# A hybrid decoder block on one core: the layout of the index phase and of the first attention's output changed, and all probability scaling of the second attention put on VectorE

## The chip, the cores and the metric

The kernel runs on one core of one Trainium2 chip. The core has five engines with a queue of their own each: TensorE (PE; its weight loads are listed as PEld), VectorE (DVE), ScalarE (ACT), GpSimd (POOL) and SyncE (SP), which here issues most DMAs. The metric is the device time of one execution in microseconds (us). Three runs of the kernel before took 1447.71 to 1451.23 us, with a median of 1449.72 us.

## The reference

One layer with 512 tokens of width 1024 in float32. The normalized input `h` goes through one wide projection, whose columns feed three token mixers and three gates. Each mixer's output is projected, gated and added to the input; then a two-layer network follows.

```python
h = rms_norm(x, norm1_g[l])
u = h @ w_in[l]
(dq, dk, dv, iq, ik, iw, nq, nkv, ng, sz, sxbc, sdt, mg) = jnp.split(u, offsets, axis=-1)
y_a = dsa_mixer(...)      # 16 heads of 64, one key/value head; an index score keeps 128 of the keys
y_b = nsa_mixer(...)      # 16 heads in 2 groups: compressed, selected and window attention, gated
y_c = ssd_mixer(...)      # 32 heads of a Mamba-2 recurrence in chunks of 128
mix = sig(g_A) * (y_a @ w_br_dsa) + sig(g_B) * (y_b @ w_br_nsa) + sig(g_C) * (y_c @ w_br_ssd)
x = x + mix @ w_out[l]
x = x + jnp.square(jax.nn.relu(rms_norm(x, norm2_g[l]) @ w_ff1[l])) @ w_ff2[l]
```

In the first attention each row's softmax `p = exp(s - max) / sum` multiplies `v`. In the second the same is done for the window and the selected blocks, and each is multiplied by a gate besides.

## The kernel before

All large products are made of three TensorE products of a high and a low half: `w = whi + wlo`, `h = hTh + hTl`, and the small product of the two low halves is dropped (L316 to L318). A weight tile of 128 rows by up to 1024 columns is loaded (`wraw`), ACT makes `whi` (L150), and DVE subtracts to give `wlo` (L151). There are 212 of these; three `wraw` and six `whi`/`wlo` are in flight, and tiles are prepared three ahead.

Two streams of work are interleaved. The main stream is: the index phase (which keys each token keeps), the first attention (DSA, 16 units of four heads by 128 queries), the recurrence (SSD), and the second attention (NSA, 32 units: 16 pairs of a window unit and a selection unit). Next to it a filler of projections supplies TensorE: `nkv`, `dq` (first-attention queries), `z`, `x`, `nq` (second-attention queries), 24 gate projections `mg`, and then the branches `a0, a1` (of y_a), `c0, c1` (of y_c), `b0, b1` (of y_b), each of four or eight `y` tiles times one weight half. After that `w_out` and the two layers of the network follow alone. The main stream books time for what it issues, and the filler is advanced until the debt is paid (`main`, `step`); a scheduler with a simulated time line then sets the order on each engine. Each engine runs its instructions in that order, and an instruction that waits holds up all behind it.

An attention unit takes these steps. Scores `sc` (L752, L753) are masked and their row maxima taken on DVE (L754); ACT makes `p = exp(...)` with the row sums (L761); DVE takes the reciprocal `rc` (L767), in NSA times the gate (L769); then `p` is scaled by `rc`, heads 0 to 2 on DVE (L774) and head 3 on POOL (L772). TensorE transposes `p` (L788), ACT and DVE make halves of it (L792, L793), and `pv` collects p times v (L800, L801). The values are laid out so that rows 0 to 63 of `pv` hold one half product and rows 64 to 127 the other; they are added as ACT copies the upper rows (L807) and DVE adds the lower ones (L808), and `yt` is stored (L809) into `ya_d` or `yb_d` in DRAM.

The branches read it back with `load_y`: SP loads `yr` (L663), ACT makes `yh` (L664), and POOL makes `yl` (L665; for `b1` DVE). `yr` comes from the tag `gt` with TG = 2 buffers, which rotate in program order and also hold `gth`, the gates' tanh (L632), stored by L633. The query blocks are transposed into `pF`; ACT and DVE make halves of 64 by 256 (L472, L473), and two DMAs of 256 KB store them in `q_d`, from which a POOL-issued DMA loads `qu` (L833).

## Time and profile before

| | before |
|---|---|
| median of three runs | 1449.72 us |
| profiled execution | 1447.78 us |
| its span, first to last instruction | 1446.1 us |
| PE busy | 1392.2 us (96%) |
| DVE busy | 973.5 us (67%) |
| ACT busy | 707.0 us (49%) |
| POOL busy | 300.1 us (21%) |
| mean granted TensorE clock | 0.982 of full speed |

The durations below are from the profiled execution, whose time is 1.7 us over its span. PE's matmuls are pipelined and their ends modelled, so that a PE shown as busy is not always at its peak: 1440 matmuls of the last 330 us take 0.229 us each, while a stretch with busy PE and slower matmuls is still listed as busy. So the number of matmuls in a stretch is read beside its busy time. The share of DVE differs greatly from stage to stage.

### The profile page before, as it was taken

Reading aid. Unit: us, or ns where it says so; the run is one execution under the profiler, and the core shown is the slowest. Engines: PE = TensorE matmul, PEld = TensorE weight load, DVE = VectorE, ACT = ScalarE, POOL = GpSimd, SP = SyncE. Lnnn points to the kernel's source line nnn. Section 1 sums busy time; section 2 is a strip of 40 time slices with the busy share of each in tenths; the row PEclk is TensorE's granted clock in tenths of the full one; section 3 lists DMA queues with packets and bytes.
Section 4 is the critical chain, followed back from the end, with each engine's and each line's share of the span. In section 5 each row is a group of like instructions: output and inputs, shape, how many; then the busy total and the mean of one; then the engine's idle time right before and its main releaser. Section 6 shows DMA issues by size and latency. Waiting matters only on the chain.

```text
span 1446.1 us, 19744 instructions
## 1 busy us (share of the span) xinstructions
PE 1392.2 (96%) x6832; PEld 1150.7 (80%) x6832; DVE 973.5 (67%) x1944; ACT 707.0 (49%) x1468; POOL 300.1 (21%) x270
## 2 busy tenths in 40 slices
PE   6999999999999989999999989998899999999998
PEld 5887778878878778788888777886679888888887
DVE  5699986888867776457578899787646443434331
ACT  4555335757756676546456446556424432413220
POOL 1021100111016767321035334252000000000000
PEclk9999999999999999999999999997899999999999
DMA  6334465454366778662277434242544323333231
GB/s 200 87 103 117 152 191 163 127 136 121 99 186 204 220 232 247 196 191 80 74 219 206 137 106 117 70 121 70 188 140 110 95 88 92 113 87 106 70 109 51
DMA packets 218273, 195.92 MB, mean 135 GB/s; under 512 B 15664, under 2 KB 165564, under 8 KB 218172
## 3 DMA queue, kind: packets, MB, share of 16 engines
q1 hardware_dynamic: 212700, 183.12, 42.8%
q0 software_dynamic: 4608, 8.39, 2.1%
q10 hardware_dynamic: 864, 3.15, 0.6%
q8 instruction: 54, 0.88, 0.3%
q14 instruction: 47, 0.39, 0.1%
HBM read 157.85 MB, written 36.77 MB: 135 GB/s over the span
## 4 chain that ended last, share of the span: by engine, by line
PE 67%; DVE 13%; DMA 9%; issue 4%; ACT 3%; POOL 3%; SPq 1%; DVEq 0%; POOLq 0%; ACTq 0%
PE pj L316 18%; PE pj L317 18%; PE pj L318 18%; DMA gld<-g_d 3%; DVE wlo L151 2%; PE pT L788 2%; PE sc L753 2%; PE sc L752 1%; DVE p L774 1%; PE pv L801 1%; PE pv L800 1%; DVE p L754 1%; DMA wraw<-in_w_in_dram 1%; DMA E<-ac_d 1%; ACT p L761 1%
## 5 line engine op out<-in xcount | busy, mean ns | idle before, releaser
L151 DVE TENSOR_TENSOR wlo<-wraw,whi 128x1024 fp32r<-128x1024 f32 (+3 forms) x212 | 257.1, 1216 | 133.3 <-ACT whi L150 124.1
L150 ACT ACTIVATE whi<-wraw 128x1024 fp32r<-128x1024 f32 (+3 forms) x212 | 207.8, 985 | 273.4 <-PE pj L317 118.5
L316 PE MATMUL pj<-hTh,whi 128*128 128x512 f32 x384 | 156.2, 407 | 0.9 <-DVE cacc L681 0.7
L318 PE MATMUL pj<-hTh,wlo 128*128 128x512 f32 x384 | 155.5, 405 | 0.0
L317 PE MATMUL pj<-hTl,whi 128*128 128x512 f32 x384 | 153.8, 401 | 0.0
L761 ACT ACTIVATE p<-p,nb,rs 128x256 f32<-128x256 f32 (+3 forms) x192 | 123.2, 644 | 58.8 <-DVE nb L759 58.8
L316 PE MATMUL pj<-whi,hTh 128*128 128x512 f32 (+2 forms) x352 | 139.5, 397 | 5.1 <-ACT qraw L458 1.7
L318 PE MATMUL pj<-whi,hTl 128*128 128x512 f32 (+2 forms) x352 | 137.9, 392 | 0.0
L317 PE MATMUL pj<-wlo,hTh 128*128 128x512 f32 (+2 forms) x352 | 137.5, 391 | 0.0
L316 PE MATMUL pj<-yh,whi 128*128 128x512 f32 x256 | 102.8, 405 | 5.0 <-ACT yh L664 3.0
L317 PE MATMUL pj<-yl,whi 128*128 128x512 f32 x256 | 102.7, 401 | 0.3 <-POOL yl L665 0.2
L318 PE MATMUL pj<-yh,wlo 128*128 128x512 f32 x256 | 101.7, 398 | 0.0
L316 PE MATMUL pj<-whi,fh 128*128 128x512 f32 x256 | 99.6, 389 | 0.0
L317 PE MATMUL pj<-wlo,fh 128*128 128x512 f32 x256 | 99.6, 389 | 0.0
L318 PE MATMUL pj<-whi,fo 128*128 128x512 f32 x256 | 99.6, 389 | 0.0
L317 PE MATMUL pj<-h2l,whi 128*128 128x512 f32 (+1 forms) x256 | 96.3, 376 | 0.0
L318 PE MATMUL pj<-h2h,wlo 128*128 128x512 f32 (+1 forms) x256 | 96.2, 376 | 0.0
L316 PE MATMUL pj<-h2h,whi 128*128 128x512 f32 (+1 forms) x256 | 96.1, 376 | 0.0
L772 POOL TENSOR_TENSOR p<-p,rc 128x256 f32<-128x256 f32 (+3 forms) x48 | 40.1, 835 | 230.3 <-DVE rc L767 88.3
L316 PEld LDWEIGHTS pj<-hTh,whi 128*128 128x128 f32 x384 | 73.0, 190 | 17.7 <-issue 2.4
L318 PEld LDWEIGHTS pj<-hTh,wlo 128*128 128x128 f32 x384 | 72.7, 189 | 16.5 <-issue 2.2
L1369 DVE TENSOR_TENSOR x<-x,pj 128x512 f32<-128x512 f32 x32 | 22.0, 686 | 93.5 <-PE pj L318 93.5
(332 smaller groups left out, 3153.0 us busy)
## 6 DMA issues: line engine op xcount, KB each, us to landing
wraw<-in_w_in_dram SPq DMA_DIRECT2D x84, 512.0 KB, 4.6
wraw<-in_w_ff_dram SPq DMA_DIRECT2D x64, 512.0 KB, 4.1
gld<-g_d SPq DMA_DIRECT2D x48, 256.0 KB, 3.5
q_d<-qev SPq DMA_DIRECT2D x32, 256.0 KB, 3.2
qu<-q_d POOLq DMA_DIRECT2D x32, 256.0 KB, 4.2
E<-ac_d SPq DMA_DIRECT2D x16, 512.0 KB, 4.9
wraw<-in_w_br_ssd_dram SPq DMA_DIRECT2D x16, 512.0 KB, 4.3
g_d<-gth SPq DMA_DIRECT2D x24, 256.0 KB, 2.4
```

The costliest lines, as they stand in the source:

```text
L150: act.activation(hi[:, :m], r[:, :m], AF.Copy)
L151: dve.tensor_tensor(lo[:, :m], r[:, :m], f(hi[:, :m]), op=ALU.subtract)
L316: pe.matmul(o, lh, rh, start=first, stop=False)
L317: pe.matmul(o, lh, rl, start=False, stop=False)
L318: pe.matmul(o, ll, rh, start=False, stop=last)
L752: pe.matmul(s_[:, h % w, :n], u.q[:, h], kh[:, :n], start=True, stop=False)
L753: pe.matmul(s_[:, h % w, :n], u.q[:, h], kl[:, :n], start=False, stop=True)
L754: dve.tensor_tensor_reduce(p_[:, h % w, :n], s_[:, h % w, :n], u.mask, 1.0, -3.4e38, ALU.add, ALU.max, accum_out=u.mx[:, h:h + 1])
L761: act.activation(u.p[h][:, :n], u.p[h][:, :n], AF.Exp, bias=u.nb[:, h:h + 1], scale=rs8[:, u.b, u.h0 + h:u.h0 + h + 1], accum_out=u.sm[:, ...
L772: pool.tensor_tensor(u.p[h][:, :n], u.p[h][:, :n], bc(rc[:, h:h + 1], [128, n]), op=ALU.mult)
L788: pe.transpose(pt[:, h], u.p[h][:, kb * 128:kb * 128 + 128], ident)
L1369: dve.tensor_tensor(x2s, x2s, p, op=ALU.add)
```

## The change

What it does, part by part:

1. The low halves `wlo` of the first 24 weight tiles (the first projection, `nkv`, `dq` and `z0`) are made on POOL instead of DVE.
2. A query block is evicted by one ACT copy and one DVE subtraction of 128 by 512 per (o, t), instead of four and four of 64 by 256. Eight DMAs of 64 rows and 512-byte pieces write it instead of two of 128 rows (16 blocks).
3. The output of the first attention is stored unscaled and unadded: ACT copies all of `pv` (128 by 512), and two DMAs write the two halves to `ya_d` and `ya2_d`. The same holds for group 0 of the second attention (`yb_d`, `yb2_d`). The DVE addition is gone there.
4. The first attention's `p` is not scaled. The reciprocals are gathered in `RC`, transposed at its end and stored in `rc_d` (`rc_out`).
5. `load_y` pays for this: for `a0`, `a1` and `b0` a POOL-issued accumulating DMA adds the second half into `yr`; for `a0` and `a1` a tile `yR` of the same tag `gt` is loaded with the reciprocals (two DMAs of 64 rows), and DVE multiplies. `yl` is made on DVE for every branch.
6. The second attention scales all four heads on DVE.
7. `ssd_prelude` is called after `nkv` instead of inside the index phase.

```diff
--- before.py
+++ after.py
@@ -24,8 +24,8 @@
 NS = 6
 RAWB = 3
 LEAD = 3
+NP = 24
 WE = 2
-SPL = {"a0": 1, "a1": 1, "c0": 1, "c1": 1, "b0": 1, "b1": 0}
 NH = 4
 BH = 2
 PTB, YTB, PGB = 3, 1, 1
@@ -78,6 +78,8 @@
     ac_d = scratch("ac_d", [128, 128])
     yc_d = scratch("yc_d", [2048, S])
     rs_d = scratch("rs_d", [4, 128])
+    rc_d = scratch("rc_d", [64, 128])
+    y2_d = {"a": scratch("ya2_d", [D, S]), "b": scratch("yb2_d", [D // 2, S])}
 
 
     cp = popen("const")
@@ -148,7 +150,7 @@
             hi = wp.tile([128, 1024], F32R, name="whi", tag="whi", bufs=NS)
             lo = wp.tile([128, 1024], F32R, name="wlo", tag="wlo", bufs=NS)
             act.activation(hi[:, :m], r[:, :m], AF.Copy)
-            dve.tensor_tensor(lo[:, :m], r[:, :m], f(hi[:, :m]), op=ALU.subtract)
+            (pool if i < NP else dve).tensor_tensor(lo[:, :m], r[:, :m], f(hi[:, :m]), op=ALU.subtract)
             s.hl[i] = (hi[:, :m].rearrange("p (a b) -> p a b", b=w), lo[:, :m].rearrange("p (a b) -> p a b", b=w))
             s.nsplit += 1
 
@@ -464,14 +466,16 @@
                 pt = ps("pF", [128, 4, 128])
                 for k in range(4):
                     pe.transpose(pt[:, k], raw[:, 128 * k:128 * k + 128], ident)
-                for j in range(2):
-                    ev = stg.tile([128, 2, 2, 128], F32R, name="qev", tag="ev", bufs=EB)
-                    pj = pt[:, 2 * j:2 * j + 2]
-                    for i in range(2):
-                        own, other = slice(64 * i, 64 * i + 64), slice(64 - 64 * i, 128 - 64 * i)
-                        act.activation(ev[own, :, i], pj[own], AF.Copy)
-                        dve.tensor_tensor(ev[other, :, i], pj[own], f(ev[own, :, i]), op=ALU.subtract)
-                    nc.sync.dma_start(q_d[2 * o + j][t], f(ev).rearrange("p a b c -> p (a b c)"))
+                qh = stg.tile([128, 4, 128], F32R, name="qev", tag="ev", bufs=EB)
+                ql = stg.tile([128, 4, 128], F32R, name="qev", tag="ev", bufs=EB)
+                act.activation(qh, pt, AF.Copy)
+                dve.tensor_tensor(ql, pt, f(qh), op=ALU.subtract)
+                for i in range(2):
+                    own, other = slice(64 * i, 64 * i + 64), slice(64 - 64 * i, 128 - 64 * i)
+                    for j in range(2):
+                        dst = q_d[2 * o + j][t].rearrange("r (a i c) -> r a i c", a=2, i=2)
+                        for e, rows in ((qh, own), (ql, other)):
+                            nc.sync.dma_start(dst[rows, :, i], f(e[own, 2 * j:2 * j + 2]))
                 if t == NB - 1:
                     done.add(f"q{o}")
             defer(0, tr)
@@ -661,8 +665,16 @@
         l_ = yp.tile([128, S], F32R, name="yl", bufs=4)
         src = yc_d if br[0] == "c" else y_d[br[0]]
         nc.sync.dma_start(yr, src[kk * 128:kk * 128 + 128])
+        if br[0] == "a" or br == "b0":
+            pool.dma_start(yr, y2_d[br[0]][kk * 128:kk * 128 + 128], accum_op=ALU.add)
+        if br[0] == "a":
+            R = gp.tile([128, S], F32, name="yR", tag="gt", bufs=TG)
+            for i in range(2):
+                a = rc_d[8 * kk + 4 * i:8 * kk + 4 * i + 4]
+                nc.sync.dma_start(R[64 * i:64 * i + 64], bass.AP(tensor=a.tensor, offset=a.offset, ap=[[0, 64], [1, S]]))
+            dve.tensor_tensor(yr, yr, R, op=ALU.mult)
         act.activation(h_, yr, AF.Copy)
-        (pool if SPL[br] else dve).tensor_tensor(l_, yr, f(h_), op=ALU.subtract)
+        dve.tensor_tensor(l_, yr, f(h_), op=ALU.subtract)
         return h_, l_
 
     def first_ya():
@@ -709,7 +721,6 @@
         for t in range(1, NB):
             IQ[t] = ix.tile([128, 8, 128], F32R, name=f"iqT{t}")
         yield "ik"
-        sv = yield from ssd_prelude()
         for b in range(1, NB):
             yield f"iq{b}"
             n = 128 * (b + 1)
@@ -731,7 +742,6 @@
             MASK[b] = wk
         MASK[0] = caus[:, 384:]
         pclose("idx")
-        return sv
 
 
     class U:
@@ -761,17 +771,26 @@
             act.activation(u.p[h][:, :n], u.p[h][:, :n], AF.Exp, bias=u.nb[:, h:h + 1],
                            scale=rs8[:, u.b, u.h0 + h:u.h0 + h + 1], accum_out=u.sm[:, h:h + 1])
 
+    RC = {}
+
+    def rc_out():
+        p = ps("pT", [128, 4, 128])
+        pe.transpose(p[:64, 0], RC["t"].rearrange("p a b -> p (a b)"), ident)
+        rt = gp.tile([128, S], F32, name="rct", tag="gt", bufs=TG)[0:64, 0:128]
+        act.activation(rt, p[:64, 0], AF.Copy)
+        nc.sync.dma_start(rc_d, rt)
+
     def a2(u):
         n = 128 * (u.b + 1)
+        if u.gate is None:
+            dve.reciprocal(RC["t"][:, u.h0:u.h0 + 4, u.b], u.sm)
+            return
         rc = at.tile([128, 4], F32, name="rc", bufs=3)
         dve.reciprocal(rc, u.sm)
         if u.gate is not None:
             dve.tensor_tensor(rc, rc, u.gate, op=ALU.mult)
         for h in range(4):
-            if h == 3:
-                pool.tensor_tensor(u.p[h][:, :n], u.p[h][:, :n], bc(rc[:, h:h + 1], [128, n]), op=ALU.mult)
-            else:
-                dve.tensor_scalar(u.p[h][:, :n], u.p[h][:, :n], rc[:, h:h + 1], None, op0=ALU.mult)
+            dve.tensor_scalar(u.p[h][:, :n], u.p[h][:, :n], rc[:, h:h + 1], None, op0=ALU.mult)
 
     def b1(u, ratio):
         nb = u.b + 1
@@ -801,7 +820,12 @@
                 pe.matmul(o, vk, pl0, start=False, stop=en)
                 yield ratio * 432
             prev = (kb, ph, pl)
-        if u.last:
+        if u.last and u.ydst2 is not None:
+            yt = at.tile([128, 4, 128], F32, name="yt", bufs=YTB)
+            act.activation(yt.rearrange("p a b -> p (a b)"), o, AF.Copy)
+            nc.sync.dma_start(u.ydst, yt[0:64])
+            nc.sync.dma_start(u.ydst2, yt[64:128])
+        elif u.last:
             yt = at.tile([64, 4, 128], F32, name="yt", bufs=YTB)
             ytf = yt.rearrange("p a b -> p (a b)")
             act.activation(ytf, o[64:128], AF.Copy)
@@ -833,8 +857,8 @@
         pool.dma_start(q.rearrange("p a b -> p (a b)"), q_d[hb][b])
         return q
 
-    def y_dst(which, h0, b):
-        t = y_d[which]
+    def y_dst(which, h0, b, ys=y_d):
+        t = ys[which]
         a = t[h0 * 64:(h0 + 4) * 64, b * 128:(b + 1) * 128]
         return a.rearrange("(h d) q -> d h q", d=64)
 
@@ -846,6 +870,7 @@
                 u.b, u.h0, u.k, u.v = b, 4 * hb, K["d"], V["d"]
                 u.gate, u.first, u.last, u.pre, u.load = None, True, True, None, None
                 u.ydst = y_dst("a", 4 * hb, b)
+                u.ydst2 = y_dst("a", 4 * hb, b, y2_d)
                 u.hb = hb
                 us.append(u)
         qs = {}
@@ -985,6 +1010,7 @@
                     u.first, u.last = kind == "w", kind == "s"
                     u.pre = cmp_pv(b, g, j) if kind == "w" else None
                     u.ydst = y_dst("b", 8 * g + 4 * j, b)
+                    u.ydst2 = y_dst("b", 4 * j, b, y2_d) if g == 0 else None
 
                     def prep(u=u, b=b, g=g, j=j, kind=kind):
                         u.q = Q[b, g][j]
@@ -1383,12 +1409,15 @@
     def main():
         nonlocal at
         HI[0] = 0
-        sv = yield from dsa_index(mk)
+        yield from dsa_index(mk)
         yield "dq"
         yield "nkv"
+        sv = yield from ssd_prelude()
         at = popen("att", side="right")
+        RC["t"] = kv.tile([128, 16, 4], F32, name="rcall")
         HI[0] = HM
         yield from pipeline(dsa_units(), R1)
+        rc_out()
         pclose("att")
         pclose("mask")
         yield from ssd(sv, R3)
```

The order of the instructions is shown at three places. `gth` is a gate tile, `yr` and `yh` a loaded `y` tile and its high half; the numbers behind the names tell buffers apart.

The first place is on ACT, where the last gate tiles meet the loads of branch `a0`. Before, it reads:

```order
L150 ACTIVATE whi_7027<-wraw_6796 128x1024
L632 ACTIVATE gth_6761<-pj_6706 128x512
L664 ACTIVATE yh_6768<-yr_6767 128x512
L150 ACTIVATE whi_7110<-wraw_6888 128x1024
L664 ACTIVATE yh_6774<-yr_6773 128x512
L664 ACTIVATE yh_6780<-yr_6779 128x512
L632 ACTIVATE gth_6880<-pj_6791 128x512
L664 ACTIVATE yh_6786<-yr_6785 128x512
L885 ACTIVATE ct_6043<-ct_6043 128x256
L150 ACTIVATE whi_7191<-wraw_6944 128x1024
L632 ACTIVATE gth_6936<-pj_6883 128x512
```

All four `yh` stand between the last instructions of the recurrence and the second attention, and one `gth` stands among them. After the change, from one `yh` to the next gate tile:

```order
L771 ACTIVATE p_6937,smx_6935<-p_6937,nb_6934,rs8_325 128x128 x4
L957 ACTIVATE cph_7095<-pF_7090 128x512
L676 ACTIVATE yh_6719<-yr_6718 128x512
L811 ACTIVATE pth_6993<-pT_6988 128x512
L811 ACTIVATE pth_7051<-pT_7046 128x512
L771 ACTIVATE p_7016,smx_7014<-p_7016,nb_7013,rs8_325 128x128 x4
L771 ACTIVATE p_7107,smx_7105<-p_7107,nb_7104,rs8_325 128x128 x4
L676 ACTIVATE yh_6730<-yr_6729 128x512
L636 ACTIVATE gth_6829<-pj_6740 128x512
L825 ACTIVATE yt_7079<-pv_6967 128x512
L811 ACTIVATE pth_7157<-pT_7152 128x512
L636 ACTIVATE gth_6885<-pj_6832 128x512
```

Here the loads stand amid the second attention's units (`p`, `pth`, `yt`), and `gth_6829` stands behind the fourth `yh`, since the four tiles and their `yR` take the two `gt` buffers in turn. On PE, 103 matmuls of attention without a projection stand between the end of `pj_6832` and the start of `pj_6888`, and 254 matmuls stand between the end of `pj_6570`, whose `gth` held the buffer that the first load takes, and that start.

The second place is on PE at the end of the second attention (`pj` is a projection, `pv` p times v). Before, the last projection of `b0` and the first instructions behind it:

```order
L316 MATMUL pj_10066<-yh_9765,whi_9974 128x512
L317 MATMUL pj_10066<-yl_9766,whi_9974 128x512
L318 MATMUL pj_10066<-yh_9765,wlo_9975 128x512
L800 MATMUL pv_10171<-pth_10181,v_w1_313 128x512
L788 MATMUL pF_10229<-ident_105,p_10151 128x128
L752 MATMUL sc_10216<-kh_w1_308,qu_9281 128x256
L753 MATMUL sc_10216<-kl_w1_309,qu_9281 128x256
L788 MATMUL pF_10229<-ident_105,p_10151 128x128
```

and the first of `b1`, after 120 matmuls of attention alone:

```order
L800 MATMUL pv_10508<-pth_10518,v_w1_313 128x512
L801 MATMUL pv_10508<-ptl_10519,v_w1_313 128x512
L800 MATMUL pv_10508<-pth_10536,v_s1_311 128x512
L801 MATMUL pv_10508<-ptl_10537,v_s1_311 128x512
L316 MATMUL pj_10567<-yh_10483,whi_10015 128x512
L316 MATMUL pj_10568<-yh_10483,whi_10067 128x512
```

After the change, the end of attention and the rest of `b0`:

```order
L819 MATMUL pv_10481<-pth_10509,v_s1_314 128x512
L820 MATMUL pv_10481<-ptl_10510,v_s1_314 128x512
L318 MATMUL pj_9745<-yh_9730,whi_9569 128x512
L318 MATMUL pj_9772<-yh_9730,whi_9638 128x512
L319 MATMUL pj_9745<-yl_9731,whi_9569 128x512
L320 MATMUL pj_9745<-yh_9730,wlo_9570 128x512
L319 MATMUL pj_9772<-yl_9731,whi_9638 128x512
```

and the first of `b1`:

```order
L318 MATMUL pj_10039<-yh_9737,whi_9947 128x512
L319 MATMUL pj_10039<-yl_9738,whi_9947 128x512
L320 MATMUL pj_10039<-yh_9737,wlo_9948 128x512
L318 MATMUL pj_10540<-yh_10456,whi_9988 128x512
L319 MATMUL pj_10540<-yl_10457,whi_9988 128x512
L320 MATMUL pj_10540<-yh_10456,wlo_9989 128x512
```

Before, `b0` is used up ahead of the last units and `b1` follows attention at once. After it, three quarters of `b0` (72 matmuls) stand between the last unit's `pv` and `b1`.

The third place is the start of POOL's queue (`rs1` normalizes a row block of the input). Before:

```order
L1019 AFFINE_SELECT pre_618<-pre_618 128x128
L272 TENSOR_TENSOR rs1_183<-ss1_182,mhalf_179 128x1 x4
L388 TENSOR_TENSOR rtk_525<-stk_522,mhalf_179 128x4
L1048 MEMSET pre_618 128x128
L492 MEMSET xc_1240 128x32
L529 MEMSET zero_1586 128x256
```

After:

```order
L274 TENSOR_TENSOR rs1_186<-ss1_185,mhalf_182 128x1
L153 TENSOR_TENSOR wlo_339<-wraw_148,whi_338 128x912
L274 TENSOR_TENSOR rs1_186<-ss1_185,mhalf_182 128x1
L153 TENSOR_TENSOR wlo_343<-wraw_152,whi_342 128x912
L274 TENSOR_TENSOR rs1_186<-ss1_185,mhalf_182 128x1
L153 TENSOR_TENSOR wlo_347<-wraw_156,whi_346 128x912
L274 TENSOR_TENSOR rs1_186<-ss1_185,mhalf_182 128x1
L153 TENSOR_TENSOR wlo_364<-wraw_350,whi_363 128x912
L153 TENSOR_TENSOR wlo_376<-wraw_353,whi_375 128x1024
```

Low halves now stand between the four `rs1`, and those of `nkv` behind them.

## Rows read from the trace of the kernel before

**Rows 1.** Page, part 1: busy time, share of span, instructions.
```profile
PE 1392.2 (96%) x6832; PEld 1150.7 (80%) x6832; DVE 973.5 (67%) x1944; ACT 707.0 (49%) x1468; POOL 300.1 (21%) x270
```
**Rows 2.** Windows: stretch, us; PE, PEld, DVE, ACT, POOL busy; clock; DMA; GB/s.
```profile
72.00:214.00 142.00, 135.71 (x692) 112.63 (x690) 132.88 (x302) 64.19 (x132) 22.58 (x18) 0.99 0.46 139
214.00:425.00 211.00, 209.12 (x1057) 174.25 (x1058) 175.56 (x378) 137.94 (x274) 20.05 (x28) 0.99 0.49 133
425.00:612.00 187.00, 177.64 (x915) 143.19 (x913) 123.54 (x151) 120.40 (x323) 120.28 (x88) 0.98 0.76 225
650.00:792.00 142.00, 142.00 (x748) 119.89 (x747) 107.68 (x272) 82.24 (x179) 35.99 (x33) 1.00 0.48 143
792.00:972.00 180.00, 171.93 (x856) 139.19 (x855) 155.02 (x349) 89.84 (x195) 71.16 (x57) 0.99 0.38 111
1116.00:1446.00 330.00, 326.39 (x1440) 269.99 (x1439) 127.65 (x148) 91.15 (x114) 0.00 (x0) 1.00 0.29 91
```
**Rows 3.** Windows at the end of the second attention; all instructions, same columns.
```profile
984.00:1016.50 32.50, 25.47 (x99) 20.16 (x99) 20.45 (x90) 19.94 (x61) 3.97 (x7) 0.63 0.22 66
1016.50:1044.00 27.50, 25.27 (x98) 19.01 (x99) 20.61 (x29) 12.78 (x18) 0.00 (x0) 0.94 0.57 184
```
**Rows 4.** The same stretch, projections (tile pj) alone.
```profile
984.00:1016.50 32.50, 0.00 (x0) 0.00 (x0) 0.00 (x0) 0.00 (x0) 0.63 0.22 66
```
**Rows 5.** Timeline near 1013 us: start, length, what, idle before and releaser.
```profile
1013.21 0.90 SPq L663 DMA_DIRECT2D yr<-yb_d  x2
1014.40 0.68 DVE L808 TENSOR_TENSOR yt<-pv,yt 64x512 f32<-64x512 f32 x1 [3.02 <-ACT yt L807]
1016.58 1.22 PE L316 MATMUL pj<-yh,whi 128*128 128x512 f32 x2 [2.84 <-ACT yh L664]
```
**Rows 6.** Groups by line, DVE, shapes apart: busy us, mean ns, idle before.
```profile
L473 DVE TENSOR_TENSOR qev<-pF,qev 64x256 fp32r<-64x256 f32 x64 | 27.0, 422 | 21.9 <-ACT qev L472 20.3
L808 DVE TENSOR_TENSOR yt<-pv,yt 64x512 f32<-64x512 f32 x32 | 21.6, 675 | 9.1 <-ACT yt L807 9.1
```
**Rows 7.** Windows of line L774 alone, first and second attention: DVE busy.
```profile
214.00:425.00 211.00, 21.64 (x48) 0.99 0.49 133
612.00:1016.50 404.50, 48.07 (x96) 0.97 0.43 127
```
**Rows 8.** Timeline, DVE and POOL beside each other near 659 and 800 us.
```profile
659.19 1.74 DVE L774 TENSOR_SCALAR p<-p,rc 128x512 f32<-128x512 f32 x3
799.52 2.31 DVE L151 TENSOR_TENSOR wlo<-wraw,whi 128x1024 fp32r<-128x1024 f32 x1
799.27 3.71 POOL L665 TENSOR_TENSOR yl<-yr,yh 128x512 fp32r<-128x512 f32 x2
640.12 1.22 DVE L151 TENSOR_TENSOR wlo<-wraw,whi 128x1024 fp32r<-128x1024 f32 x1
```
**Rows 9.** Tile yr: its users' durations min/median/max, and its loads.
```profile
L664 ACT ACTIVATE yh<-yr x32: 615/632/646, 625.7 to 1021.1; 128x512 fp32r<-128x512 f32 x32
L665 DVE TENSOR_TENSOR yl<-yr,yh x4: 691/692/693, 1016.6 to 1021.8; 128x512 fp32r<-128x512 f32 x4
L665 POOL TENSOR_TENSOR yl<-yr,yh x28: 1288/1354/2271, 628.1 to 956.4; 128x512 fp32r<-128x512 f32 x28
```
**Rows 10.** DMA issues: what, count, KB each, median us to landing; then tile qu.
```profile
qu<-q_d POOLq DMA_DIRECT2D x32, 256.0 KB, 4.2
yr<-ya_d SPq DMA_DIRECT2D x8, 256.0 KB, 4.2
g_d<-gth SPq DMA_DIRECT2D x24, 256.0 KB, 2.4
...
DMA to landing us min/median/max: 2.8/4.2/6.1
```
**Rows 11.** Waits of PE by total, 792 to 972 us: total, times, longest.
```profile
PE pT L788 <- DVE p L774: 4.4, 3, 3.0
```

## The prediction, written before the changed kernel ran

> **What bounds the kernel now.** I read the page's busy times first. PE is busy for 1392.2 of 1446.1 us [rows 1], so only what PE loses can be won: the idle 53.9 us, the time at a lower clock (0.018 of 1446 = 26 us), and matmuls that stand apart though the engine counts as busy. Then the windows by stage, where the reader is to set DVE's busy time beside PE's. In the index stage DVE is busy for 132.88 of 142 us and in the first attention for 175.56 of 211 [rows 2]; both are DVE's stages. To size what PE loses there I take the stage of the gate projections, 650 to 792 us, where PE is busy throughout: 748 matmuls in 142 us, 0.190 us each [rows 2]. At that rate index would take 692 x 0.190 = 131.5 us (10.5 less), the first attention 200.8 (10.2 less), the second from 792 to 972 us 162.6 (17.4 less). Shapes differ, so these are estimates, and upper bounds of what lighter DVE work can give. Last I read the end of the second attention. From 984 to 1016.5 us PE is busy 25.47 us at clock 0.63 [rows 3], and no projection runs [rows 4]: 25.47 x 0.63 = 16.0 us of work at full speed in 32.5, 16.5 lost. From 1016.5 to 1044 us there are 98 matmuls [rows 3], nearly all of 512 columns; at 330/1440 = 0.229 us [rows 2] they need 22.4 of 27.5, 5.1 lost. The granted clock, half speed for part of that time, rose only once projections ran again. The timeline shows why: `yr` is issued at 1013.21, the last addition of `yt` runs at 1014.40 and `b1` begins at 1016.58 [rows 5]. So about 22 us are lost because `b0` was used up before attention ended.
>
> **The change part by part.**
>
> *Low halves on POOL.* A POOL subtraction of 128x512 takes 1.354 us in the median, one on DVE 0.692 [rows 9]; so one of 1024 costs POOL about 2.7 us where DVE takes 1.22 [rows 8]. 24 of these are some 24 x 1.22 = 29 us off DVE and 24 x 2.5 = 60 on POOL, which is busy for 22.58 us in the index stage. Against it: beside a POOL subtraction the same instruction on DVE took 2.31 instead of 1.22 us [rows 8], 1.1 us lost. If each of the 24 did that, 26 of the 29 us return. I count nothing for this part; the ends are -6 and +5 us (the `rtk` and `rs1` now queue behind low halves on POOL, each up to 2.7 us).
>
> The Trainium skill says in "SBUF — State Buffer", section "Who interferes with whom", that a VectorE instruction with two SBUF inputs contends with a GpSimd one that reads SBUF, and that the later one blocks for the whole instruction. The 2.31 us beside the 3.71 us pair [rows 8] agree: 1.1 us lost there, over half of one POOL instruction of 1.85. By the rule a DVE instruction waits on the average for half of a POOL low half of 2.7 us; were each met once, 24 x 1.35 = 32 us would be lost for 29 saved, which is rival D.
>
> *Query eviction.* 64 DVE pieces of 0.422 us [rows 6] become 16 of 0.692: 27.0 - 11.1 = 16 us off DVE, half of it in the index stage, half in the recurrence (DVE 123.54 of 187, not its bound). The price is 96 more DMAs on SP, at 0.32 us of SP's time as `yr` loads show (0.90 for two with gaps [rows 5] is the upper end, 43 us over both stages); weight loads queue behind them, three tiles ahead. Index: -3 us (ends +5, -10.5 with the part above). Recurrence: -2 (ends +5 and -9, the idle there [rows 2]).
>
> *First attention.* Its scaling took DVE 21.64 us [rows 7] and 16 additions of `yt` 16 x 0.675 = 10.8 [rows 6]: 32.4 of 175.56 us go. The chain max, exp, scale, transpose becomes shorter by a step. I take -7 of the 10.2 us; the ends are 0 (projections hid it) and -10.2.
>
> *Second attention.* The fourth head comes to DVE. But the three of 128x512 that DVE does beside POOL's took 1.74 us [rows 8], and the mean over all sizes is 48.07/96 = 0.50 [rows 7]. DVE gains at most 32 x 0.50 = 16 us, 28 `yl` of 0.692 = 19.4 and 8 multiplications of about 0.69 = 5.5, and loses 8 x 0.675 = 5.4: +35.5 over 360 us. POOL's 28 `yl` and 32 scalings, each of which could hold up DVE by up to 1.1 us [rows 8], are gone. The transposes wait for the scaling for 4.4 us in all [rows 11]. I take -4, between -17 and +10 (10 being a second such wait twice over in a stage that is busy for 155.02 of 180 us [rows 2]).
>
> *End of the second attention.* In the new order 72 matmuls of `b0` stand between attention and `b1`, 72 x 0.229 = 16.5 us; the store and the reload of the last `y` are two transfers, for which the POOL loads' 2.8 to 6.1 us each [rows 10] are the nearest row. So the 22 us go. What is late next is the start of `b0` itself, whose second pair of tiles waits for two `gt` buffers, an SP load and an accumulating POOL DMA: +5, between 0 and 10. Net -17 (ends 0 and -22).
>
> *Loads of `a0` and `a1`.* Here the change adds a wait. Two `gt` buffers used to hold two `yr`, so that two tiles were under way; now each tile takes both (`yr`, `yR`), and the tiles follow one another. A cycle: SP load 4.2 us [rows 10]; accumulating POOL DMA, which the trace does not show, between 2.8 (the fastest POOL DMA) and 8.4 (twice 4.2, since it reads the tile and writes it), taken as 5, near the POOL DMA's 4.2 [rows 10]; multiplication 0.69; `yh` 0.632 and `yl` 0.692 [rows 9]; and about 1.8 of queueing on DVE, ACT, POOL and SP, where attention's instructions stand in between. 4.2 + 5 + 0.7 + 0.6 + 0.7 + 1.8 = 13 us, ends 9.5 and 17.5. Behind the fourth tile stands `gth_6829`, and behind that the next projection. Four cycles, and about 12 us of lead (the last gate's projection, tanh, store of 2.4 us and load of `yR`), are 64 us. PE has 254 matmuls for it, 254 x 0.190 = 48 us. Lost: 16 us. `a1` does it again, with about 4 us of lead and about as much cover (the 96 matmuls of `a0` and attention): 4 + 52 - 48 = 8. Together 8c - 80 for a cycle of c, 24 us at 13; at 9.5 none, at 17.5 60.
>
> The Trainium skill ("DMA: Bandwidth & Descriptors", section "Anatomy of one DMA — SWDGE (gpsimd) path") fits a POOL-issued DMA by 2.0 us plus the bytes over 436 GB/s, 2.6 us for this tile. The trace does not agree: 4.2 in the median for the same bytes [rows 10]. By the fit the cycle would be 10.6 us, the loss 5 and the whole some 19 us less.
>
> *The sum.* -3 - 7 - 2 - 4 - 17 + 24 = -9 us against the profiled 1447.8: 1438.8. The median of the runs is 1.9 us above the profiled one, so 1441 is what I expect of a median. The prelude's new place costs nothing: its instructions stay where they stood in the order.
>
> **The rivals.**
>
> *B: the loads of `y_a` cost more than all the rest gives.* The two `gt` buffers make the cycle serial, and VectorE and ScalarE hold attention's instructions behind each step. It decides where 8c - 80 exceeds the 33 us gained, at c = 14.1 us, little above my 13. For it: the accumulating DMA may take 8.4. Against: 13 already holds 1.8 us of queueing, and every part of it that the trace shows is a median. At c = 16.5 the loss is 52 us: 1447.8 + 52 - 33 + 1.9 = 1469.
>
> *C: the end of attention gains nothing.* The units are a chain, the last ones run without projections just as before, and `b0` only stands later. For it: half clock in that stretch. Against: projections now stand among the last units. Then -17 is missing: 1458.
>
> *D: POOL's low halves hold up DVE in the index stage, and DVE's added work costs in the second attention.* Then index and second attention give +3 and +4 instead of -3 and -4: 14 us more, 1455.
>
> *E: the loads are fast.* A cycle near 10 us leaves nothing lost: 24 us less, 1417.
>
> **How the numbers follow.** Forecast 0.52, B 0.18, C 0.07, D 0.08, E 0.15. A measurement here tells 0.2%, 2.9 us, from no change. The forecast's own range is 1428 to 1454. Faster: 0.41 of the forecast, all of E, 0.02 of D: 0.58. Same: 0.09 of the forecast, 0.01 each of C and D: 0.11. Slower: 0.02 of the forecast, B's 0.18, 0.06 of C, 0.05 of D: 0.31. The range is 1412 to 1468: E's side is in but for its far end, and B's upper half is out.
>
> **What would show it.** Right: in the gates' stage, ahead of the gate tile behind the fourth `yh`, some 16 us that PE loses; `yr` followed by an accumulating DMA, with the four tiles about 13 us apart; DVE near 140 us in the first attention; no stretch of 30 us without a projection at the end. Wrong: tiles 9 or 17 us apart, or DVE's subtractions near 2.3 us all through the index stage. The accumulating DMA's time to landing is what would refute the forecast first.

## The result, and the profile after

The changed kernel takes 1462.91 us in the median of four runs (1459.67 to 1464.98) where the kernel before takes 1448.72: 1.0095 of it, with a 95% interval of 1.0071 to 1.0119. It is slower. The forecast was 1441 us, faster; the time lies inside the stated range of 1412 to 1468 us, but on the slower side of no change.

The page of the changed kernel, as in [rows 1]:

```profile
PE 1396.5 (95%) x6833; PEld 1150.8 (79%) x6833; DVE 918.5 (63%) x1868; ACT 687.3 (47%) x1421; POOL 280.5 (19%) x230
```

VectorE (DVE) has 55 us less to do, and that bought nothing: the span is 1463.3 us. To see where, one needs more than busy times. For each matmul I took the time since the start of the matmul before it. From it I subtracted the time below which the quickest fifth of such times lie, over the runs compared, behind a matmul of the earlier one's shape and output tile. Then I added that up by stretches. I call it PE's loss. The work of PE is the same in both kernels, so differences of loss are differences of time:

| stretch, us from start | before | after | difference | my term |
|---|---|---|---|---|
| 0 to 216, index | 31.8 | 41.5 | +9.7 | -3 |
| 216 to 396, first attention | 23.8 | 20.5 | -3.3 | -7 |
| 396 to 504, recurrence, first half | 18.7 | 26.9 | +8.2 | -2 (both halves) |
| 504 to 612 | 25.8 | 25.7 | -0.1 | |
| 612 to 720, loads of a0 | 10.8 | 27.6 | +16.8 | +16 |
| 720 to 972, second attention, loads of a1 | 38.6 | 39.9 | +1.3 | +8 - 4 |
| 972 to 1116, its end | 37.7 | 21.3 | -16.4 | -17 |

The sum is +16.2 us, the spans differ by 17.2. (This is the slowest of the four runs; the medians differ by 14.2 us.) Two limits of this table matter below. Each kernel has one profiled execution, and e4 below, which leaves the index phase as it was, reads 3 us less there than the kernel before, so differences of 3 us mean little. And the stretches are cut at fixed times while the stages move: the recurrence's first matmul starts at 431 us before and at 399 us after.

The windows after; the first stretch also for the kernel before, which [rows 2] has only as a part of a longer one (columns as in [rows 2]). First before, 72 to 180 us:

```profile
72.00:180.00 108.00, 103.14 (x546) 86.30 (x545) 103.72 (x247) 52.89 (x113) 20.22 (x14) 0.98 0.41 123
```

and after, the same stretch, then the first attention from its first scores on:

```profile
72.00:180.00 108.00, 96.69 (x513) 79.75 (x512) 106.28 (x251) 46.33 (x96) 46.87 (x26) 0.94 0.48 123
...
197.00:402.00 205.00, 204.87 (x1037) 169.91 (x1037) 137.07 (x297) 131.76 (x272) 11.28 (x17) 1.00 0.55 151
```

In the index phase PE gets through 33 fewer matmuls in the same 108 us, though low halves run on POOL now; DVE is busier than before (106.28 us for 103.72) and POOL twice as busy. In the first attention DVE falls to 137 of 205 us, from 175.56 of 211 [rows 2], and PE, which was busy already, gains little. PE's waits of the changed kernel, 60 to 216 us (who waited for whom: us in all, times, longest):

```profile
PE pj L318 <- DVE stk L388: 3.2, 1, 3.2
PE pT L1089 <- DVE sv_acm L1078: 3.1, 1, 3.1
PE pj L318 <- DVE zo L578: 2.9, 1, 2.9
```

The first is the key normalization; L1089 is a transpose of the prelude, in its new place, and `zo` is a tile of the projection `z`. Next, the loads of `a0` on SP, cut to `yr` and `yR` (start us, length):

```profile
644.02 0.52 SPq L667 DMA_DIRECT2D yr<-ya_d  x1
657.90 1.18 SPq L674 DMA_DIRECT2D yR<-rc_d  x2
664.04 0.33 SPq L667 DMA_DIRECT2D yr<-ya_d  x1
670.17 1.13 SPq L674 DMA_DIRECT2D yR<-rc_d  x2
676.37 0.34 SPq L667 DMA_DIRECT2D yr<-ya_d  x1
...
687.27 0.34 SPq L667 DMA_DIRECT2D yr<-ya_d  x1
```

The tiles are 20.0, 12.3 and 10.9 us apart. The window of that stretch, projections alone:

```profile
669.00:698.00 29.00, 0.44 (x2) 0.31 (x2) 0.00 (x0) 0.58 (x1) 0.68 0.62 141
```

So a stretch of 29 us without a projection, with the granted clock down to 0.68, has appeared ahead of the gate tile behind the fourth `yh`. The one at the end of the second attention [rows 4] is gone: from the last product with `v`, at 1007.5 us, the span goes on for 455.8 us, where before it was 433.4 from 1012.7. Attention ends 5 us earlier, and what follows it takes 22 us more, with the rest of `b0` in it.

### The profile page after: what moved, and what is told of

It is laid out like the page before. It is cut to its first block, busy times and chain, and to the rows that moved or that the text cites. A ratio compares the mean times of both kernels' runs of the same rounds, so it can differ in the third digit from the quotient of the medians.

```text
span 1463.3 us, 19709 instructions
## 1 busy us (share of the span) xinstructions
PE 1396.5 (95%) x6833; PEld 1150.8 (79%) x6833; DVE 918.5 (63%) x1868; ACT 687.3 (47%) x1421; POOL 280.5 (19%) x230
## 4 chain that ended last, share of the span: by engine, by line
PE 62%; DVE 14%; DMA 13%; issue 3%; POOL 3%; ACT 2%; SPq 2%; DVEq 0%; POOLq 0%; ACTq 0%
PE pj L318 17%; PE pj L319 17%; PE pj L320 17%; DMA gld<-g_d 3%; DMA wraw<-in_w_in_dram 2%; DVE wlo L153 2%; PE pT L807 2%; DMA yR<-rc_d 2%; POOL mixf L1309 1%; DMA yr<-ya_d 1%; PE sc L763 1%; PE sc L762 1%; PE pv L820 1%; PE pv L819 1%; DVE p L793 1%
## 5 line engine op out<-in xcount | busy, mean ns | idle before, releaser
L153 DVE TENSOR_TENSOR wlo<-wraw,whi 128x1024 fp32r<-128x1024 f32 (+1 forms) x188 | 224.7, 1196 | 132.8 <-ACT whi L152 128.8
L318 PE MATMUL pj<-yh,whi 128*128 128x512 f32 x256 | 102.9, 408 | 10.9 <-ACT yh L676 5.6
L318 PEld LDWEIGHTS pj<-whi,hTh 128*128 128x128 f32 x352 | 69.1, 196 | 22.1 <-issue 6.2
L319 PEld LDWEIGHTS pj<-hTl,whi 128*128 128x128 f32 x384 | 73.3, 191 | 16.3 <-issue 1.9
```

What stands on the lines that cost most here:

```text
L153: (pool if i < NP else dve).tensor_tensor(lo[:, :m], r[:, :m], f(hi[:, :m]), op=ALU.subtract)
L318: pe.matmul(o, lh, rh, start=first, stop=False)
L319: pe.matmul(o, lh, rl, start=False, stop=False)
```

## The experiments

Ratios are to the kernel before, run on the same chip, with 95% intervals. First the parts alone, on the kernel before.

**e4, the second attention's part.** Head 3 of NSA and all `yl` go to DVE.

```diff
-            if h == 3:
+            if h == 3 and u.gate is None:
-SPL = {"a0": 1, "a1": 1, "c0": 1, "c1": 1, "b0": 1, "b1": 0}
+SPL = {"a0": 0, "a1": 0, "c0": 0, "c1": 0, "b0": 0, "b1": 0}
```

> The kernel before (1448.7 us) with two edits alone: the second attention's fourth head scaled on VectorE, and all low halves of y on VectorE. My step: 4 us gained (1445), from POOL no longer holding up VectorE. Rival: VectorE was not what PE waited for, 0 (1449 within 3), with the end of the second attention losing its 22 us as before.

0.9941 [0.9922, 0.9960], 1435.3 us: twice the 4 us of my term. The scaling of a tile of 128x512 in e4, which [rows 8] shows at 1.74 us for three beside POOL's:

```profile
L774 DVE TENSOR_SCALAR p<-p,rc 128x512 f32<-128x512 f32 x44 | 22.2, 560 | 0.3
```

Its mean was 790 ns before. PE's transposes, which from 612 to 972 us waited 4.4 us for the scaling [rows 11], wait 0.2 us in e4. In the changed kernel, where POOL scales nothing in either attention, the 128 scalings of the second take 42.3 us in all, less than the 48.07 that 96 took before [rows 7].

**e8, the query eviction.** The change's lines in `q_block`, alone.

```diff
+                act.activation(qh, pt, AF.Copy)
+                dve.tensor_tensor(ql, pt, f(qh), op=ALU.subtract)
```

> The kernel before with the new query eviction alone (one copy and one subtraction, eight DMAs a block). Theory: VectorE's 16 us less are worth nothing in the index stage, and the queue of SP costs up to 7 us in the recurrence: 1.003 to 1.005. My forecast's step: 0.997. Both seen from 396 to 504 us, where the kernel before loses about 19 us against matmuls in close sequence.

0.9939 [0.9914, 0.9964], against both what I expected here (a loss) and the size of my term (-3 and -2). The loss from 0 to 216 us falls from 32 to 24 us. In the recurrence the theory's sign is seen, at a part of its size: 20.8 us of loss from 396 to 504, 18.7 before, and PE's waits there for `bcx`, which SP loads, come to 3.4 us for 1.1. That these waits come from the 96 more DMAs on SP is not shown.

**e9 and e10, both, and b0's unadded halves with them.** e9 is e4's and e8's edits together. e10 adds:

```diff
+        if br == "b0":
+            pool.dma_start(yr, y2_d[br[0]][kk * 128:kk * 128 + 128], accum_op=ALU.add)
+                    u.ydst2 = y_dst("b", 4 * j, b, y2_d) if g == 0 else None
```

> The kernel before with the two parts that gained when alone: second attention's scaling and low halves on VectorE, and the new query eviction. Theory: while the projections run out before attention ends, the time is attention's end plus a fixed rest of 432 to 434 us, so whatever moves attention's end counts in full: 1012.7 before, 1001 and 1004 in the two parts; both together 993, or 0.987 of the kernel before. Rival: both shorten the same waits, 0.994, attention ending near 1001.

> The same with group 0's values of the second attention unadded and the accumulating DMA for b0's tiles. Theory: the end of attention moves by little, and b0's start gets a wait of up to 5 us which the 30 us without projections at the end cover: within 0.3% of the kernel without it. Rival: the start of b0 and SP's two more stores per unit delay attention: 0.5% slower than without it.

Both 0.9901 (e9 0.9877 to 0.9925, 1429.67 us; e10 0.9878 to 0.9925). e9 lies between its theory and its rival: the two gains mostly add. Attention ends at 997 and 994 us, and the rest stays at 432 and 436. The unadded halves of `b0` move nothing. e10's stretch without projections at the end is still there (tile pj alone):

```profile
966.00:996.00 30.00, 0.00 (x0) 0.00 (x0) 0.68 (x1) 0.00 (x0) 0.82 0.25 75
```

So `b0`'s part alone does not remove it, and e9 and e10 beat both kernels.

**e12, the first attention's part.** Index phase, second attention and `SPL` as before.

```diff
+            dve.reciprocal(RC["t"][:, u.h0:u.h0 + 4, u.b], u.sm)
+                u.ydst2 = y_dst("a", 4 * hb, b, y2_d)
+            dve.tensor_tensor(yr, yr, R, op=ALU.mult)
```

> The kernel before with the first attention's part alone: p unscaled, halves unadded, reciprocals and accumulating DMA in the loads of a0 and a1. The index phase, the second attention and its low halves on GpSimd are as before. Theory: a stretch of 20 us or more without projections at the loads of a0; the projections that are missing there are left over at the end and fill the stretch of 37 us without projections, but attention does not end earlier by as much: 1.005 to 1.010. Rival: VectorE's relief of 32 us in the first attention brings attention's end forward by 7 us or more: 1.000 or less.

1.0193 [1.0150, 1.0236], worse than expected. In its profile 24.1 us go without a projection at `a0`'s loads, and attention ends at 1038 us.

Then the changed kernel with parts undone, each diff the reverse of the part named.

**e1 (low halves), e2 (prelude), e5 (query eviction), e6 (all three).**

```diff
-NP = 24
+NP = 0
```

```diff
         yield "ik"
+        sv = yield from ssd_prelude()
-        yield from dsa_index(mk)
+        sv = yield from dsa_index(mk)
-        sv = yield from ssd_prelude()
```

```diff
+                        act.activation(ev[own, :, i], pj[own], AF.Copy)
+                        dve.tensor_tensor(ev[other, :, i], pj[own], f(ev[own, :, i]), op=ALU.subtract)
```

> The changed kernel (1462.9 us) with all low halves of weights on VectorE again. Theory: low halves in POOL's queue delay the small POOL operations of the index stage (key normalization at 96 us waits 3.3 us) and the clock falls after; then the 5 us that 72 to 108 us lose more than before come back, about 1458 us. Rival: VectorE, busy for 35 of 36 us there, is what bounds that stretch, and with 24 more subtractions of 1.22 us (29 us) it gets later: 1466 us or more.

> The changed kernel with the recurrence's prelude inside the index phase as before. Theory: the two stops of PE of 3.3 us at 166 and 169 us, on the prelude's sums, and the half clock behind them come from its new place: about 8 us back, 1455 us, and no such stops from 140 to 185 us. Rival: they only move to another place of the stage, 1463 us within 3.

> The changed kernel with the query blocks evicted and stored as before (four and four pieces of 64 by 256, two DMAs a block). Theory: the eight DMAs a block, 96 more in all, stand on SP's queue before the recurrence's loads and cost about 7 us from 396 to 504 us, where every version with them loses more than the kernel before: 0.5% under the changed kernel, 1.005 of the kernel before. Rival: that stretch loses its time to something else (the order of the recurrence against z and x), and VectorE's 16 us come back: 1.010 to 1.015 of the kernel before.

> The changed kernel with all three edits of the index phase undone: low halves on VectorE, the prelude inside the index phase, the old query eviction. What is left are the edits of the attentions' outputs and of the scaling. Theory: the index edits cost 7 + 5 + 7 us and add up: about 0.996 of the kernel before. Rival: each only moves a stop that then falls elsewhere, as with the prelude alone: 1.009.

They gave 1.0099 [1.0076, 1.0122], 1.0152 [1.0127, 1.0177], 1.0057 [1.0033, 1.0081] and 1.0146 [1.0117, 1.0175]. The theories of e1, e2 and e6 have the right sign up to 216 us and failed in the total. There e1 loses 7 us less, e2 5 us less, e6 12 less; the ratio does not fall, since at the end they lose more again (22, 26 and 30 us from 972 to 1044, where the changed kernel loses 16). e5 came out in the total where its theory put it (1.0057 for 1.005), but not by that stretch alone: from 396 to 504 us it loses 2 us less, from 504 to 612 us 6 less, and up to 216 us 5 more. These runs are inconclusive on what an edit costs.

**e3 (reciprocals undone), e11 (a's accumulating DMA undone), e7 (e3 and e6 together).**

```diff
-            dve.tensor_tensor(yr, yr, R, op=ALU.mult)
-            dve.reciprocal(RC["t"][:, u.h0:u.h0 + 4, u.b], u.sm)
-            return
```

```diff
-        if br[0] == "a" or br == "b0":
+        if br == "b0":
-                u.ydst2 = y_dst("a", 4 * hb, b, y2_d)
+                u.ydst2 = None
```

> The changed kernel with the first attention's p scaled again (all four heads on VectorE), so that no tile of reciprocals is loaded and multiplied and two y tiles of a0 and a1 are under way at once; the accumulating DMA stays. Theory: the serial loads through two buffers cost the 17 us that 612 to 720 us lose more than before, and the scaling taken off VectorE (some 25 us) gave PE at most 2: about 1448 us. Rival: the accumulating DMA is the cost, whichever buffers there are: 1458 us or more. Second rival: VectorE's relief in the first attention is worth the 7 us that I forecast, and the gain is 10 only: 1453 us.

> The changed kernel with the first attention's halves added by VectorE again, so that y_a is loaded without an accumulating DMA; the tile of reciprocals and its buffer stay. Theory: the cycle of the y tiles falls from 11 to 12 us by the accumulating DMA's 4.3 and its queueing to 6 or 7, the stretch without projections from 29 us to 15 or less: 1.004 of the kernel before. Rival: the buffers alone make the stretch, the first load's lead of 20 us above all: 25 us or more without projections, and 1.009.

> The same, and the first attention's p scaled on VectorE (four heads), without the tile of reciprocals. Theory: the loads of a0 and a1 then lose nothing either and what is left is the second attention's part with the unadded halves: about 0.990 of the kernel before, near the 0.994 of the second part alone. Rival: the unadded halves with the accumulating DMA cost as much as that part gives: 1.000.

e3 1.0055 [1.0039, 1.0071], e11 1.0002 [0.9981, 1.0023], e7 0.9988 [0.9969, 1.0007]. Without `yR` the stretch at `a0` has projections again (tile pj, e3):

```profile
640.00:662.00 22.00, 14.02 (x52) 8.92 (x50) 0.00 (x0) 1.18 (x2) 1.00 0.69 166
```

The loss from 612 to 720 us falls back to about 10 us in e3, as before the change; the total falls by 0.4% only, since the end loses 10 us more again. With `yR` but without the accumulating DMA the stretch stays, shorter (19 us in e11). e11's tiles stand 9.7 and 8.8 us apart, not 6 or 7. So the buffers make the stretch. What the DMA adds to a cycle is not shown: e13 below, without it, has cycles of 11.4 to 11.7 us. e7 came out at its rival's figure.

**e13 to e16, one edit added to e10.** The four edits by which the changed kernel differs from e10, each alone: reciprocals, unadded halves of `y_a`, low halves on POOL, the prelude after `nkv`. The diffs are those above, forward.

> The 0.990 version (e10) with the first attention's reciprocals held back to the loads of a0 and a1, its halves added as before. Theory: a stretch of about 20 us without projections at a0's loads costs 12 to 16 us against matmuls in close sequence, and what is left over there fills the stretch at the end: 0.995 to 1.003 of the kernel before. Rival: the scaling that VectorE no longer does brings attention's end forward and the end gives all back: 0.990 or less.

> The 0.990 version with the halves of y_a unadded and the accumulating DMA in a0's and a1's loads, p scaled as before. Theory: two y tiles are under way at once, so a0's loads leave no stretch of over 10 us without projections; 16 more stores on SP before the recurrence's loads cost a few us from 396 to 504: 0.993 to 0.997. Rival: the accumulating DMA alone is the cost: 1.000 or more.

> The 0.990 version with the low halves of the first 24 weight tiles on GpSimd. Theory: POOL's queue delays the small operations of the key normalization, about 5 us lost from 72 to 108 us, and as attention's end sets the time, it counts: 0.993. Rival: VectorE's 29 us in the index stage count, 0.985.

> The 0.990 version with the recurrence's prelude after nkv. Theory: two stops of 3.3 us from 140 to 180 us, about 7 us with the half clock behind them, but the index phase that decides the first attention's start ends earlier, as in the changed kernel (197 us for the first scores against 214): 0.988 to 0.993. Rival: the earlier start of attention brings its end forward by more than 7 us, 0.985 or less.

| | ratio to before | above e10 | loss 0-216 | 612-720 | 972-1116 |
|---|---|---|---|---|---|
| e10 | 0.9901 [0.9878, 0.9925] | | 23.9 | 11.2 | 31.8 |
| e13, reciprocals | 1.0023 [1.0009, 1.0037] | +1.2% | 22.9 | 26.7 | 34.8 |
| e14, halves of y_a | 0.9949 [0.9930, 0.9968] | +0.5% | 23.2 | 17.7 | 33.5 |
| e15, low halves on POOL | 0.9957 [0.9936, 0.9978] | +0.6% | 36.9 | 11.3 | 28.5 |
| e16, prelude later | 1.0002 [0.9986, 1.0018] | +1.0% | 33.0 | 10.3 | 29.1 |
| the changed kernel | 1.0095 [1.0071, 1.0119] | +1.9% | 41.5 | 27.6 | 21.3 |

Each edit costs. The times of e13 and e14 lie in the range of their theories; the low halves and the prelude cost more than expected. (The profiled execution of e13 is 6 us above its median, that of e16 5 us below, so their losses are not as exact as their ratios.) The four add up to 3.3%, all four together cost 1.9%, some 20 us less; 10 us of that are in the end's stretch, which loses that much less in the changed kernel than in e10. The windows from 72 to 180 us, in the order e10, e15, e16:

```profile
72.00:180.00 108.00, 107.26 (x577) 89.86 (x576) 103.23 (x245) 50.03 (x98) 21.18 (x14) 1.00 0.53 145
```

```profile
72.00:180.00 108.00, 98.96 (x530) 82.42 (x529) 103.98 (x232) 47.92 (x98) 47.97 (x26) 0.97 0.47 126
```

```profile
72.00:180.00 108.00, 100.02 (x532) 83.25 (x531) 102.43 (x247) 48.45 (x94) 18.55 (x14) 0.95 0.48 128
```

With the low halves DVE does fewer instructions (232 for 245) in the same busy time, and PE 47 matmuls less. The reason can be read from the rows. First one operation of the key normalization in that window, in e10 and in e15, then in e15 one of its four, beside POOL:

```profile
L387 DVE TENSOR_SCALAR stk<-stk 128x4 f32<-128x4 f32 x4 | 0.6, 160 | 0.0
```

```profile
L388 DVE TENSOR_SCALAR stk<-stk 128x4 f32<-128x4 f32 x4 | 3.8, 956 | 0.0
```

```profile
98.65 2.39 POOL L153 TENSOR_TENSOR wlo<-wraw,whi 128x1024 fp32r<-128x1024 f32 x1
99.32 1.75 DVE L388 TENSOR_SCALAR stk<-stk 128x4 f32<-128x4 f32 x1
```

The instruction of 0.16 us lasts until POOL's subtraction ends. Five kinds of DVE instructions (`stk`, `ssq`, `sqk` and two of `mask`) are drawn out so, by some 13 us in all, where 13 subtractions fewer save 16. From 60 to 200 us PE waits for `qev`, `v_w` and `v_s`, which DVE makes, 9.1 us in all, and for nothing that POOL makes. So it is the hold-up of DVE that is seen, from 108 us on above all, and not POOL's queue, which my theory had.

The later prelude costs as much with POOL quiet. Its waits in e16, 60 to 200 us:

```profile
PE pj L318 <- DVE zo L578: 4.1, 1, 4.1
PE pT L1070 <- DVE vz L543: 3.2, 1, 3.2
```

L1070 is the first product of the prelude. e10 has one wait of 0.7 us there. In e13 the stretch at `a0`, tile pj alone:

```profile
637.00:663.00 26.00, 0.00 (x0) 0.06 (x1) 0.00 (x0) 0.57 (x1) 0.87 0.32 91
```

## Why the prediction was wrong

**The step that failed** is the treatment of the index phase, two of its lines. "The prelude's new place costs nothing: its instructions stay where they stood in the order" holds for the long chain on DVE, which starts at 48.2 us before and 49.6 after. It is wrong on PE, where the prelude's first product moves from 61.5 to 162.6 us. There it and the projection behind it wait for DVE, and e16 shows 1.0%, some 15 us. "I count nothing for this part" of the low halves was 0.6% by e15, some 8 us. Rival D had named the hold-up of DVE behind it. The query eviction gave 8 us in this stretch (e8), and still the index term came out at +9.7 instead of -3. The next largest miss, the recurrence, has no settled cause (below).

**The Trainium skill's rule** on the ports ("SBUF — State Buffer", "Who interferes with whom") pointed the right way: by it I had worked out 32 us lost for 29 saved, and set it aside as a rival. In e15 DVE's busy time is 103.98 us against 103.23 with 13 instructions fewer. The trace agrees with the sign.

**Right as to the mechanism, and in size partly by luck:** the loads of `a0`. 16 us were forecast, 16.8 measured. e3 and e13 show that the reciprocals' tile in the two buffers makes it. But the terms differ. The wait that the sum has at 64 us, from the end of the projection it starts with (640.5) to the next projection (697.8), took 57.3. And the 254 matmuls that cover it, many of them short ones of attention, need 35 us at the quick rate of their kinds, not 48. The cycles were 12.3 and 10.9 us for my 13, and are made otherwise. The load of `yR`, which the sum has in the lead alone, stands in every cycle, and the accumulating DMA runs beside it. In the changed kernel the second and the fourth multiplication, with what they waited for:

```profile
675.65 0.69 DVE L675 TENSOR_TENSOR yr<-yr,yR 128x512 f32<-128x512 f32 x1 [0.95 <-DMA yR<-rc_d]
694.84 0.69 DVE L675 TENSOR_TENSOR yr<-yr,yR 128x512 f32<-128x512 f32 x1 [1.73 <-DMA yr<-ya_d]
```

For the first three tiles the accumulating DMA had landed 10.6, 4.5 and 2.7 us before the multiplication; only the fourth waited for it. So its time to landing, which I had named as what would refute the forecast first, decided little.

For `a1` I had 8 us. The stretch 720 to 972 changes by +1.3 in all, but e4's edits alone take some 6 us off it, and the changed kernel, which has them, shows no such gain. So a cost of some 7 us can be in there; no run shows it by itself.

**Right in size, wrong in what it means:** the end. -17 was forecast, -16.4 measured. But I gave it to `b0`'s new halves, and e10, which has them, keeps its 31.5 us without projections. In the changed kernel the projections that fill the end are, as far as I can tell, those that were not done earlier. That is time given back in part, not a gain of that edit, so adding it to the other terms as if it were its own was a mistake. The runs show which kernels do it: the span goes on for 454 to 456 us after attention in the changed kernel, e5 and e11, which all have the low halves on POOL, the later prelude and `yR`. With one of the three undone (e1, e2, e3) it is 433 to 441 us. Why it takes all three was not settled.

**Too small:** the second attention and the query eviction. They gave 0.6% each alone, some 8.6 us each, for my 4 and 5. For the first the shorter scalings and the transposes' waits that went show a cause; the low halves `yl`, changed in the same run, were not tried apart.

**Open:** the first attention's relief, -7 for -3.3 in the table. Counted by its own time (214 to 431 us before, 197 to 399 after) the same measure gives -6.5, but e8, which leaves these steps as they were, gives -4.3 there, and e12, which has this part alone, -4.9. How much belongs to the relief is not shown, although DVE is busy for 38 us less.

**Not foreseen:** the recurrence, -2 for +8.2 from 396 to 504 us. Its earlier start is not the reason: by its own time, from its first matmul to its last (431 to 607 us before, 399 to 584 after), it loses 10 us more. PE's longest waits in that stretch of the changed kernel are for `bcx` loads (5.5 us in two). The query eviction is a suspect: by the recurrence's own time it adds 5 us in e8, and undoing it takes 9 off in e5. But e14 and e15 have it too and lose at most 2 us more there than the kernel before. The cause stays open.

## What to carry to other kernels

Taking work off a busy engine pays only if what takes its place elsewhere does not hold that engine up; 13 instructions fewer at the same busy time is how that reads. Two buffers that gain a second user per step turn an overlapped load into a chain, and every load on that chain has to be found, since a sum can come out right with one left out and one too many. Where two streams share one engine, undoing one edit at a time misleads, since what is lost early is in part given back late: build up from the version that is best, one edit at a time.

## What the runs showed of the hardware

The accumulating POOL DMA landed nearly as fast as a plain one, 4.3 us for 256 KB in the median where the plain `qu` took 3.9, but it holds POOL longer to issue (0.886 us for 0.537, medians of the changed kernel). The changed kernel's rows, issues and then tile yr:

```profile
yr<-ya_d POOLq DMA_DIRECT2D x8, 256.0 KB, 4.3
```

```profile
L669 POOL DMA_DIRECT2D yr<-ya_d x8: 863/886/905, 648.7 to 823.5; - x8
```

A DMA of 64 KB in pieces of 512 bytes took 2.3 us to land in the changed kernel where one of 256 KB took 3.2 in the kernel before (medians). With four times as many of them e8 still gained 0.6%. Beside a POOL subtraction of 2.39 us a DVE instruction of 0.16 us took 1.75 us (e15).
